# Moving TensorE's operands by 32 bytes, and letting small tiles share memory

## The chip, the cores and the metric

The kernel runs on one NeuronCore of a Trainium2 chip. It is one launch, and the time is the device time of that launch in microseconds (us). Everything is fp32 at the interface.

Five engines work side by side: TensorE (PE in the profile, with its weight loads as PEld), VectorE (DVE), ScalarE (ACT), GpSimd (POOL) and SyncE (SP, which here only issues DMAs). SBUF, the on-chip memory, has 128 partitions. A tile occupies the same bytes of every partition, so "the position of a tile" is one byte number.

## The reference

One layer of a streaming encoder runs over 1024 prompt tokens and 64 sample tokens (T = 1088 columns), with a model width of 1024:

```
xn  = rms_norm(x, g_attn)
rq, rk, rv, rg, sq, sk, sv, ga, gb = split(xn @ w_in)
A   = rms_norm(retention(rope(rq), rope(rk), rv)) * silu(rg) @ w_ret_out     # 4 heads of 256
B   = sliding_window_attention(sq, sk, sv, rel_bias, sinks) @ w_swa_out      # 16 heads of 64
x  += (sigmoid(ga) * A + sigmoid(gb) * B) @ w_mix_out
x  += softmax((rms_norm(x) @ w_cq) @ mk.T) @ mv @ w_co                       # 256 memory tokens
x  += (silu(rms_norm(x) @ w_gate) * (rms_norm(x) @ w_up)) @ w_down           # hidden size 2816
y   = rms_norm(x, g_final)
```

The outputs are `y`, the retention states, the window's keys and values, and the keys and values of the memory tokens (`mk`, `mv`).

## The kernel before, in words

**The matmuls.** Activations lie transposed: 128 features on the partitions, tokens along the columns. A number of fp32 precision is split into two parts, `hi` (rounded by a cast on ScalarE, L123) and `lo = x - hi` (on VectorE, L124). A product is three matmuls: weights' hi by operand's hi, hi by lo, lo by hi (`mm3`, L147 to L151, and `multiply`, L197 to L209). In each, one 128 x 128 block of weights is the stationary operand, loaded by an LDWEIGHTS of its own, and 256 to 384 columns of the operand move past it.

**Two families of tiles feed them.** The weights' parts come from `new_op` (L144): a tile `wq` of 2 x 512 floats, 4096 bytes, with hi in the first half and lo in the second. There are five such buffers in the projection phase and six in the later ones (`self.weights(5)`, `self.weights(6)`), used in turn. The moving operands stand in two rings of eight slots, 2 x 1088 floats or 8704 bytes each (`Ring`, L98): the names `B11` to `B22` and `T1` to `T4` (printed as `B` and `T`), `ret`, `swa`, `mix`, `xc`, `co`, `stage` and `swin` in the profile are all slots of the rings.

**The phases, in order.** The projections run from 0 to about 820 us as Strassen products of 2 x 2 blocks (`strassen`, L247; seven products instead of eight), each product a run of 272-column matmuls. Between them lie the retention of the four heads (`retention`, L702) and, near the end, the memory's keys and values (`memory_phase`, L482). Then come the window attention with `w_ret_out` as filler, `w_swa_out` and `w_mix_out` (320 and 384 columns), cross attention (`w_cq`: 256 and 320 columns), `w_co`, and from about 1500 us the feed-forward network, again as Strassen products of 272 columns. A scheduler orders the instructions of each engine at build time from the dependences between tiles.

**Where the tiles stand.** Pools of the left side are stacked from byte 0 upward, pools of the right side from byte 229344 downward. Every tile takes a multiple of 32 bytes. Before the change:

- the `wq` buffers start at byte 16320 and every 4096 bytes after that, all at a multiple of 64;
- the 16 ring slots start at byte 90080 and every 8704 bytes after that. 90080 = 1407 * 64 + 32, and 8704 = 136 * 64, so all slots stand at byte 32 of 64. Inside a slot the parts used are 1088, 2176 and 4352 bytes apart or start 1024, 1536, 2048 or 3072 bytes in, all multiples of 64, so that every moving operand in the rings starts at byte 32 of 64;
- the retention's operands (`ks`, `qs`, `kt`, `vb`, `ss`, `st`) and cross attention's (`mkv`, `cqs`, `cpT`) are on the left, all at a multiple of 64;
- the memory's operands `ms` are on the right below the rings, at byte 32 of 64;
- `b12`, the block `B12` of the first product of the projections and of the feed-forward network (printed as `b`), is on the left in the first case (byte 45504, a multiple of 64) and on the right in the second (byte 32 of 64).

So the pairs of residues that a matmul meets (moving operand, weights; byte of 64) are (32, 0) for all ring products, (0, 0) in retention and cross attention and for the first `b12`, (32, 0) where `ms` moves past `wq` (`w_mk`) and (0, 32) where `wq` moves past `ms` (`w_mv`; there the weights' tile is the moving operand). Both parts of an operand always have the same residue. In the last phase (`finish`) weights stand in ring slots too (`wb`), which makes (32, 32).

**Room.** In the retention's phase the left side ends at byte 90048 and the rings begin at 90080; in the memory's phase the left side ends at 73664 and `ms` begins at 73696. 32 bytes are free in each.

**The small tiles.** At the end of each head, `retention` handles the 64 sample tokens: it loads keys `kf` (tag `sf`), values `vf` and queries `qf` (tag `qsm`), and keeps a masked score in `sf` (tag `sfs`). `memory_phase` loads the memory's raw columns into `mraw` (two buffers) and puts results into `mo` (four buffers).

Of the kernel before, what the change touches and what calls it, by code (L numbers as in the profile page):

```python
# [11 lines left out]
F32 = mybir.dt.float32  # L12
F32R = mybir.dt.float32r
# [6 lines left out]
P = 128  # L20
# [3 lines left out]
SMP = 64  # L24
# [6 lines left out]
NMEM = 256  # L31
# [78 lines left out]
class Kernel:  # L110
# [31 lines left out]
        return parts  # L142

    def new_op(self):  # L144
        return self.wp.tile([P, 2, 512], F32R, tag="wq", bufs=self.wbufs, name="wq")

    def mm3(self, ps, wh, wl, xh, xl, start, stop):  # L147
        mm = self.nc.tensor.matmul
# [184 lines left out]
    def run(self):  # L333
        nc, tc, io = self.nc, self.tc, self.io
        with ExitStack() as ctx:
            cp = ctx.enter_context(tc.tile_pool(name="const", bufs=1, reuse_waits="tile"))
            self.np = ctx.enter_context(tc.tile_pool(name="norm", bufs=1, reuse_waits="tile"))
            dp = ctx.enter_context(tc.tile_pool(name="scratch", bufs=1, reuse_waits="tile", space=DRAM))

            self.ident = cp.tile([P, P], F32, name="ident")  # L340
            self.ones = cp.tile([P, P], F32, name="ones")
            self.gains = cp.tile([P, 5, KT], F32, name="gains")
            self.load(self.gains, io["g_all"])
            nc.vector.memset(self.ones, 1.0)
            self.rstd = cp.tile([P, T], F32, name="rstd")
            nc.scalar.mul(self.rstd[:, :1], self.ones[:, :1], 1.0)

            self.root = cp.tile([P, len(CH), 3], F32, name="root")
            self.rtok = cp.tile([P, 9], F32, name="rtok")
            nc.vector.memset(self.rtok, 1.0)  # L350
            self.mtok = cp.tile([P, 2], F32, name="mtok")
            self.tab = cp.tile([P, 2, H, 3], F32, name="tab")
            self.tok = cp.tile([P, 3, H, 9], F32, name="tok")
            self.sinks = cp.tile([P, NPAIR], F32, name="sinks")

            self.d_mk = dp.tile([H, P, 2, NMEM], F32, name="d_mk")
            self.d_mv = dp.tile([H, P, 2, NMEM], F32, name="d_mv")
            self.d_ret = dp.tile([KT, P, T], F32, name="d_ret")
            self.d_swa = dp.tile([KT, P, T], F32, name="d_swa")
            self.d_gate = [dp.tile([KT, P, T], F32, name=f"d_gate{i}") for i in range(3)]  # L360
            self.d_mix = dp.tile([KT, P, T], F32, name="d_mix")
            self.d_h = [dp.tile([KT, P, T], F32, name=f"d_h{i}") for i in range(2)]
            self.d_op = dp.tile([len(OPS), FT // 2, P, HALF], F32, name="d_op")
            self.d_rb = dp.tile([16, 64 * 256], F32, name="d_rb")

            self.d_qkv = dp.tile([3, KT, P, T], F32, name="d_qkv")
            self.d_skv = dp.tile([2, P, T], F32, name="d_skv")
            self.d_sq = dp.tile([NPAIR // 2, P, 17, 2, 64], F32, name="d_sq")

            with ExitStack() as sctx:  # L370
                self.rings = [Ring(sctx.enter_context(tc.tile_pool(name=f"ring{i}", bufs=1, reuse_waits="tile", side="right")))
                              for i in range(2)]
                self.mem = sctx.enter_context(ExitStack())
                with self.weights(5):
                    self.project_phase()
                with self.weights(6):
                    with self.plain_psum():
                        self.mix_phase()
                        self.mem.close()
                        self.cross_phase()  # L380
                    rp = sctx.enter_context(tc.tile_pool(name="rf", bufs=1, reuse_waits="tile", side="right"))
                    self.rstd_f = rp.tile([P, T], F32, name="rstd_f")
                    self.temp = sctx.enter_context(ExitStack())
                    self.new_b12(self.temp, side="right")
                    self.cross_out_phase()
                    self.ffn_phase()
# [95 lines left out]
    def memory_phase(self, mp):  # L482


        nc, tc, io = self.nc, self.tc, self.io
        g_mem = self.gains[:, 4, :]
        mr = self.mem.enter_context(tc.tile_pool(name="mr", bufs=1, reuse_waits="tile", side="right"))
        ms = self.ms = [mr.tile([P, 2, NMEM], F32R, name=f"ms{k}") for k in range(KT)]
        macc = mp.tile([P, NMEM], F32, name="macc")
        out = lambda: mp.tile([P, NMEM], F32, tag="mo", bufs=4, name="mo")  # L490
        room = lambda: mp.tile([P, 1024], F32, tag="mw", bufs=3, name="mw")
        for k in range(KT):
            x = mp.tile([P, NMEM], F32, tag="mraw", bufs=2, name="mraw")
            self.load(x, io["memT"][:, k, :])
            self.gained(ms[k], 0, NMEM, x, g_mem, k)
            if k:
                nc.scalar.activation(x, x, AF.Square)
                nc.vector.tensor_tensor(out=macc, in0=macc, in1=x, op=ALU.add)
            else:
                nc.scalar.activation(macc, x, AF.Square)  # L500
            if k % 2:
                yield
        self.token_rstd(self.mtok, [macc], self.spans(NMEM), D)
        yield
        self.spread(macc, self.mtok)
        for m in range(KT):
            ps = self.dense(self.unit(io["w_mk"][m], KT, room=room), ms, 0, NMEM)
            o = out()
            nc.vector.tensor_tensor(out=o, in0=ps, in1=macc, op=ALU.mult)
            self.store(self.d_mk[m // 2, :, m % 2, :], o)  # L510
            self.store(io["o_mk"][m], o)
            yield
        for h in range(H - 1):
            us = [self.unit(io["w_mv"][h, i], 4, 256, room) for i in range(2)]
            for t in range(2):
                ps = self.dense_psum()
                for k in range(KT):
                    x = ms[k][:, :, t * P:(t + 1) * P]
                    self.mm3(ps[:, :256], x[:, 0], x[:, 1], *us[k // 4][k % 4], k == 0, k == KT - 1)
                o = out()  # L520
                nc.scalar.mul(o, ps[:, :256], self.mtok[:, t:t + 1])
                self.store(self.d_mv[h, :, t, :], o)
                self.store(io["o_mv"][t * P:(t + 1) * P, h * 256:(h + 1) * 256], o)
            yield
# [177 lines left out]
    def retention(self, h):  # L702
        nc, io = self.nc, self.io
        mm = nc.tensor.matmul
        ra = self.ra
# [7 lines left out]
        for b in range(NBLK):  # L713
# [28 lines left out]
            sf = ra.tile([P, BLK + P], F32, tag="sf", bufs=1, name="sf")  # L742
# [31 lines left out]
        self.store(io["o_rsp"][h].rearrange("(t p) e -> p t e", p=P), state)  # L774

        s0, vf = new("state"), new("vf")
        kf, qf = (ra.tile([P, 2, SMP], F32, tag=tag, bufs=1, name=tag) for tag in ("sf", "qsm"))
        self.load(s0, io["cstate"][h].rearrange("(t p) e -> p t e", p=P))
        vf = vf[:, :, :SMP]
        for j, x in ((1, kf), (2, vf), (0, qf)):  # L780
# [6 lines left out]
        pss = self.bank("psss")  # L787
        for dt in range(2):
            mm(pss[:SMP, 0, :SMP], kf[:, dt, :], qf[:, dt, :], start=dt == 0, stop=dt == 1)
        sf = ra.tile([P, SMP], F32, tag="sfs", bufs=1, name="sfs")  # L790
        nc.vector.scalar_tensor_tensor(sf[:SMP], pss[:SMP, 0, :SMP], self.rtok[:SMP, 8:], dm[:SMP, BLK + P:],
                                       ALU.mult, ALU.mult)
        po = self.bank("pos")
# [903 lines left out]
```

## Time and profile before

| | |
|---|---|
| median of 3 runs | 2240.6 us (2237.51 to 2248.04) |
| the profiled execution's own time | 2239.58 us |
| its span, first to last instruction | 2237.8 us |
| PE busy | 2171.3 us, 97% of the span |
| DVE, ACT, POOL busy | 72%, 40%, 31% |
| mean granted TensorE clock | 0.986 |

An instruction's row shows its line, engine and operation, then the tiles it writes and reads. For a matmul the PSUM bank stands left of the arrow; right of it the moving operand is named first and the stationary one second. A matmul's duration (about 0.29 us) is longer than the distance to the next one (about 0.12 us), since they are pipelined. The rate at which TensorE works is read from the distance between starts, which the timeline shows with a resolution of 10 ns.

### The profile page before, as it was taken

How to read it: one execution, taken by the hardware profiler on the slowest of the kernel's cores; microseconds unless marked ns; L12 is line 12 of the kernel's file. 1: busy time of each engine (PE TensorE's matmuls, PEld its weight loads, DVE VectorE, ACT ScalarE, POOL GpSimd, SP SyncE). 2: the span in 40 equal slices, each digit the busy share in tenths (PEclk: the TensorE clock that was granted, in tenths of full speed). 3: DMA queues.
4: the chain of work that ended last, by engine and by line, in shares of the span. 5: the costliest groups of instructions: out<-in, count | busy, mean ns of one | idle time of the engine just before them, and what ended most of it. 6: DMA issues, size and time to landing. Idle time of an engine off the chain costs nothing.

```text
span 2237.8 us, 41757 instructions
## 1 busy us (share of the span) xinstructions
PE 2171.3 (97%) x16434; PEld 2106.8 (94%) x16434; DVE 1600.4 (72%) x2655; ACT 884.7 (40%) x1897; POOL 690.5 (31%) x466
## 2 busy tenths in 40 slices
PE   9999999999999989999999999999999999999996
PEld 9899999999999977779999998999999999999986
DVE  8986878676687668876455555668777777778588
ACT  7333333435444355553133333333222222334243
POOL 1441533342253112220000000014555555434462
PEclk9999999999999999999999999999999999999998
DMA  5433345443445475326443112422332332475233
GB/s 205 156 111 110 117 123 137 133 127 113 167 152 178 151 229 169 114 75 208 130 154 107 55 48 65 134 85 88 122 130 101 102 122 89 142 273 182 84 102 109
DMA packets 182599, 290.86 MB, mean 130 GB/s; under 512 B 40290, under 2 KB 110850, under 8 KB 182402
## 3 DMA queue, kind: packets, MB, share of 16 engines
q1 hardware_dynamic: 177794, 279.26, 39.3%
q10 hardware_dynamic: 4608, 8.91, 1.1%
q8 instruction: 130, 2.13, 0.4%
q14 instruction: 67, 0.55, 0.1%
HBM read 196.95 MB, written 91.16 MB: 129 GB/s over the span
## 4 chain that ended last, share of the span: by engine, by line
PE 75%; DVE 7%; DMA 4%; issue 1%; ACT 1%; POOL 1%; SPq 0%; DVEq 0%; ACTq 0%; POOLq 0%
PE pq L208 14%; PE pq L206 14%; PE pq L205 14%; PE pd L149 7%; PE pd L151 7%; PE pd L150 7%; PE pout L1000 1%; DMA hl<-d_op 1%; PE pp L984 1%; DVE wq L124 1%; PE pss L942 1%; DMA ld<-d_swa 1%; DVE B L124 1%; DMA raw<-w_ret_out 1%; PE pk L699 0%
## 5 line engine op out<-in xcount | busy, mean ns | idle before, releaser
L124 DVE TENSOR_TENSOR wq<-raw,wq 128x512 fp32r<-128x512 f32 (+1 forms) x505 | 450.1, 895 | 124.8 <-ACT wq L123 122.6
L123 ACT CAST wq<-raw 128x512 fp32r<-128x512 f32 (+1 forms) x505 | 307.6, 614 | 569.9 <-PE pq L208 262.7
L205 PE MATMUL pq<-T,wq 128*128 128x272 f32 x1832 | 493.9, 289 | 6.2 <-DVE u L252 3.6
L206 PE MATMUL pq<-T,wq 128*128 128x272 f32 x1832 | 493.9, 289 | 0.0
L206 PE MATMUL pq<-B,wq 128*128 128x272 f32 x1592 | 429.3, 289 | 8.4 <-DVE B L124 8.4
L205 PE MATMUL pq<-B,wq 128*128 128x272 f32 x1592 | 426.7, 288 | 0.0
L208 PE MATMUL pq<-T,wq 128*128 128x272 f32 x1832 | 384.4, 290 | 3.4 <-DVE wq L124 3.4
L183 POOL TENSOR_TENSOR raw<-raw 128x512 f32<-128x512 f32 (+1 forms) x59 | 79.4, 1345 | 894.8 <-DVE rs_r L291 483.8
L205 PEld LDWEIGHTS pq<-T,wq 128*128 128x128 f32 x1832 | 346.7, 189 | 7.1 <-DVE u L252 3.7
L206 PEld LDWEIGHTS pq<-T,wq 128*128 128x128 f32 x1832 | 346.8, 189 | 0.3 <-issue 0.3
L208 PE MATMUL pq<-B,wq 128*128 128x272 f32 x1592 | 334.0, 290 | 0.0
L206 PEld LDWEIGHTS pq<-B,wq 128*128 128x128 f32 x1592 | 300.7, 189 | 10.3 <-DVE B L124 10.0
L205 PEld LDWEIGHTS pq<-B,wq 128*128 128x128 f32 x1592 | 300.1, 189 | 0.7 <-issue 0.4
L208 PEld LDWEIGHTS pq<-T,wq 128*128 128x128 f32 x1832 | 292.0, 191 | 4.6 <-DVE wq L124 3.8
L208 PEld LDWEIGHTS pq<-B,wq 128*128 128x128 f32 x1592 | 253.5, 190 | 0.5 <-issue 0.3
L252 DVE TENSOR_TENSOR u<-pq,u 128x544 f32<-128x544 f32 x177 | 127.5, 720 | 111.7 <-PE pq L208 111.1
L186 POOL TENSOR_TENSOR raw<-raw 128x512 f32<-128x512 f32 (+1 forms) x59 | 85.3, 1446 | 125.2 <-DVE wq L124 122.6
L970 POOL TENSOR_TENSOR t<-t,den 128x768 f32<-128x768 f32 (+2 forms) x34 | 47.8, 1406 | 167.7 <-DVE den L968 49.9
L571 DVE TENSOR_TENSOR stage<-pq,u 128x544 f32<-128x544 f32 x112 | 80.3, 717 | 26.6 <-PE pq L208 25.8
L184 POOL TENSOR_TENSOR raw<-raw 128x512 f32<-128x512 f32 (+1 forms) x59 | 89.2, 1512 | 3.7
L1455 POOL TENSOR_TENSOR y<-u,y 128x544 f32<-128x544 f32 x38 | 62.6, 1658 | 72.4 <-DVE y L1453 54.4
L189 POOL TENSOR_TENSOR raw<-raw 128x512 f32<-128x512 f32 (+1 forms) x59 | 83.2, 1411 | 4.4
(373 smaller groups left out, 4674.2 us busy)
## 6 DMA issues: line engine op xcount, KB each, us to landing
hl<-d_op SPq DMA_DIRECT2D x85, 272.0 KB, 4.4
d_qkv<-stage SPq DMA_DIRECT2D x44, 272.0 KB, 2.3
d_op<-stage SPq DMA_DIRECT2D x44, 272.0 KB, 2.1
d_op<-ht SPq DMA_DIRECT2D x44, 272.0 KB, 3.3
raw<-w_gate SPq DMA_DIRECT2D x22, 512.0 KB, 3.5
raw<-w_up SPq DMA_DIRECT2D x22, 512.0 KB, 3.6
d_gate<-stage ACTq DMA_DIRECT2D x32, 272.0 KB, 2.8
raw<-w_down SPq DMA_DIRECT2D x16, 512.0 KB, 4.4
```

The source lines that it names most:

```text
L123: self.last_cast = self.nc.scalar.copy(hi, src).ins
L124: return self.nc.vector.tensor_tensor(out=lo, in0=src, in1=hi.bitcast(F32), op=ALU.subtract).ins
L149: mm(ps, wh, xh, start=start, stop=False)
L150: mm(ps, wh, xl, start=False, stop=False)
L151: self.last_mm = mm(ps, wl, xh, start=False, stop=stop).ins
L184: tt(out=a21, in0=a21, in1=a22, op=add)
L186: tt(out=a11, in0=a22, in1=a11, op=sub)
L189: tt(out=a12, in0=a12, in1=a11, op=sub)
L205: mm(ps[:, c, :HC], w[:, 0, ks], x[:, 0, cs], start=start, stop=False)
L206: mm(ps[:, c, :HC], w[:, 0, ks], x[:, 1, cs], start=False, stop=False)
L208: self.last_mm = mm(ps[:, c, :HC], w[:, 1, ks], x[:, 0, c * HC:(c + 1) * HC], start=False, stop=stop).ins
L252: add = lambda out, a, b: nc.vector.tensor_tensor(out=out, in0=a, in1=b, op=ALU.add)
```

## The change

Three things are done:

1. A tile `edge` of 8 floats (32 bytes) is allocated on the right before the rings and never used. All that lies below it on the right moves down by 32 bytes. The ring slots, `ms` and the second `b12` then start at a multiple of 64.
2. A `wq` buffer becomes 1032 floats (4128 bytes), and the parts start 32 bytes into it. With the first buffer at 16320 the parts start at 16352 (byte 32 of 64), the next at 20480 (byte 0), and so on by turns. The pairs of the ring products become (0, 32) in buffers 0, 2 and 4 and (0, 0) in buffers 1, 3 and 5. What lies above the buffers on the left moves up by 160 bytes with five of them (a residue of 32 instead of 0: retention's operands become (32, 32)) and by 192 bytes with six (residues as before).
3. To make room, `mraw` takes its buffers from `mo`'s four, and `kf`, `qf` and the masked score become parts of one tile `small` under the tag `sf`. That frees 2048 bytes in the memory's phase and 768 in the retention's.

No instruction is added or removed.

```diff
     def new_op(self):
-        return self.wp.tile([P, 2, 512], F32R, tag="wq", bufs=self.wbufs, name="wq")
+        q = self.wp.tile([P, 1032], F32R, tag="wq", bufs=self.wbufs, name="wq")
+        return q[:, 8:8 + 1024].rearrange("p (a b) -> p a b", a=2)
...
             with ExitStack() as sctx:
+                edge = sctx.enter_context(tc.tile_pool(name="edge", bufs=1, reuse_waits="tile", side="right"))
+                edge.tile([P, 8], F32, name="edge")
                 self.rings = [Ring(sctx.enter_context(tc.tile_pool(name=f"ring{i}", bufs=1, reuse_waits="tile", side="right")))
...
         for k in range(KT):
-            x = mp.tile([P, NMEM], F32, tag="mraw", bufs=2, name="mraw")
+            x = mp.tile([P, NMEM], F32, tag="mo", bufs=4, name="mraw")
             self.load(x, io["memT"][:, k, :])
...
         s0, vf = new("state"), new("vf")
-        kf, qf = (ra.tile([P, 2, SMP], F32, tag=tag, bufs=1, name=tag) for tag in ("sf", "qsm"))
+        small = ra.tile([P, 5, SMP], F32, tag="sf", bufs=1, name="small")
+        kf, qf, sf = small[:, :2], small[:, 2:4], small[:, 4]
...
-        sf = ra.tile([P, SMP], F32, tag="sfs", bufs=1, name="sfs")
         nc.vector.scalar_tensor_tensor(sf[:SMP], pss[:SMP, 0, :SMP], self.rtok[:SMP, 8:], dm[:SMP, BLK + P:],
```

## The prediction

> **What bounds the kernel now.** The page comes first: its span, the busy times, the granted clock and the chain that ended last.
>
> ```profile
> span 2237.8 us, 41757 instructions
> PE 2171.3 (97%) x16434; PEld 2106.8 (94%) x16434; DVE 1600.4 (72%) x2655; ACT 884.7 (40%) x1897; POOL 690.5 (31%) x466
> PEclk9999999999999999999999999999999999999998
> PE 75%; DVE 7%; DMA 4%; issue 1%; ACT 1%; POOL 1%; SPq 0%; DVEq 0%; ACTq 0%; POOLq 0%
> ```
>
> TensorE is busy for 97% of the span at a granted clock of 0.9 or more in all slices but the last, and three quarters of the chain are its own instructions. The groups by line, with different shapes kept apart, show which.
>
> ```profile
> L205 PE MATMUL pq<-T,wq 128*128 128x272 f32 x1832 | 493.9, 289 | 6.2 <-DVE u L252 3.6 <-DVE B L124 1.2 <-ACT wq L123 0.8
> L206 PE MATMUL pq<-B,wq 128*128 128x272 f32 x1592 | 429.3, 289 | 8.4 <-DVE B L124 8.4
> L149 PE MATMUL pd<-xc,wq 128*128 128x256 f32 x192 | 54.3, 283 | 0.0
> L149 PE MATMUL pd<-ret,wq 128*128 128x384 f32 x128 | 46.4, 362 | 5.1 <-ACT wq L123 5.1
> L149 PE MATMUL pd<-co,wq 128*128 128x320 f32 x64 | 19.9, 312 | 0.0
> L149 PE MATMUL pd<-ms,wq 128*128 128x256 f32 x64 | 17.9, 280 | 0.0
> L205 PE MATMUL pq<-b,wq 128*128 128x272 f32 x32 | 9.6, 316 | 0.5 <-ACT rstd_f L331 0.5
> ```
>
> Each Strassen matmul occurs once in L205, L206 and L208, so there are 3 x (1832 + 1592 + 32) = 10368 ring products of 272 columns. `xc` adds 3 x 192 = 576 of 256 columns, the four operands `ret`, `swa`, `mix`, `co` give 4 x 3 x 128 = 1536 of 384, and with `xc` 5 x 3 x 64 = 960 of 320. Waits ahead of them are 0 to 8 us a group: the time is the matmuls' own pace. One nanosecond on each of the 10368 is 10.4 us.
>
> What the change can do is therefore read from the pace, that is from starts in the timeline, at stretches with different pairs of residues (moving operand, weights).
>
> ```profile
> 1640.28 0.29 PE L205 MATMUL pq<-T,wq 128*128 128x272 f32 x1
> 1655.21 0.29 PE L205 MATMUL pq<-T,wq 128*128 128x272 f32 x1
> ...
> 35.20 0.29 PE L205 MATMUL pq<-b,wq 128*128 128x272 f32 x1
> 37.46 0.29 PE L206 MATMUL pq<-B,wq 128*128 128x272 f32 x1
> 67.42 0.29 PE L206 MATMUL pq<-B,wq 128*128 128x272 f32 x1
> ...
> 692.09 0.28 PE L149 MATMUL pd<-ms,wq 128*128 128x256 f32 x1
> 695.59 0.28 PE L149 MATMUL pd<-ms,wq 128*128 128x256 f32 x1
> 756.37 0.28 PE L149 MATMUL pd<-wq,ms 128*128 128x256 f32 x1
> 761.34 0.28 PE L149 MATMUL pd<-wq,ms 128*128 128x256 f32 x1
> ...
> 143.29 0.28 PE L149 MATMUL pkv<-vb,kt 128*128 128x256 f32 x1
> 144.60 0.28 PE L151 MATMUL pkv<-vb,kt 128*128 128x256 f32 x1
> ```
>
> In order: 120 ring matmuls of 272 columns with (32, 0) take 14.93 us, 124.4 ns each. The first `b12`, (0, 0), takes 2.26 us for 18, or 125.6; the ring products behind it, (32, 0) again, take 29.96 us for 240, or 124.8. At 256 columns `ms` past `wq`, (32, 0), takes 3.50 us for 30, or 116.7; `wq` past `ms`, (0, 32), takes 4.97 us for 42, or 118.3; the retention's (0, 0) takes 1.31 us for 11, or 119.1. The pair of today is the quickest at both widths.
>
> **The change part by part.** *Ring products, 272 columns.* Their pair goes from (32, 0) to (0, 0) in half of the buffers and (0, 32) in the other half. Equal residues cost 125.6 - 124.8 = 0.8 ns against the same phase's own pace, 1.2 against the later one; I take 0.8, the neighbour with the same work beside it. No row shows (0, 32) at this width. At 256 columns it costs 1.6 where equal residues cost 2.4, two thirds, so I take 0.5 here; the bounds are the most that 256 columns show, 2.4, on the slow side and the same amount below nothing, since nothing excludes a pair quicker than today's. Sum: 5184 x 0.8 + 5184 x 0.5 = 4.1 + 2.6 = 6.7 us.
>
> *The other ring products.* 256 columns (`xc`): 288 x 2.4 + 288 x 1.6 = 1.2 us. 320 and 384 columns, 2496 of them, have only (32, 0) rows; between the mean of 272 columns (0.65) and that of 256 (2.0) I take 1.3, or 3.3 us, with 1.6 and 5.0 as ends. `w_mk` (`ms` past `wq`, 192) goes to (0, 0) and (0, 32): 96 x 2.4 + 96 x 1.6 = 0.4 us. `w_mv` (192) goes from (0, 32) to (32, 0) and (0, 0) by turns: 96 x (-1.6) + 96 x 0.8, nothing. All of this lies on the path: no other engine fills it.
>
> *Retention and `finish`.* Retention's operands go from (0, 0) to (32, 32) and `wb` from (32, 32) to (0, 0): equal before and after. I put nothing on them; cross attention keeps (0, 0).
>
> *Other engines' operands* move by 32 bytes too.
>
> ```profile
> L252 DVE TENSOR_TENSOR u<-pq,u 128x544 f32<-128x544 f32 x177 | 127.5, 720 | 111.7 <-PE pq L208 111.1
> L571 DVE TENSOR_TENSOR stage<-pq,u 128x544 f32<-128x544 f32 x112 | 80.3, 717 | 26.6 <-PE pq L208 25.8 <-ACT ret_o L819 0.7
> ```
>
> `u` stands at byte 0 of 64 and `stage` at byte 32, and the same addition takes 720 and 717 ns. So VectorE shows no price, and none is set; VectorE is busy 72% beside TensorE's 97%, and 3 ns on 289 instructions would be 0.9 us under that cover. If the cover failed it would be 0.9 us.
>
> *Small tiles.* What is queued and who waits:
>
> ```profile
> L117 SPq DMA_DIRECT2D qsm<-d_qkv x4: 360/374/388, 100.4 to 457.8; - x4
> DMA to landing us min/median/max: 2.0/2.5/4.4
> L117 SPq DMA_DIRECT2D sf<-d_qkv x4: 359/360/360, 196.5 to 547.0; - x4
> L789 PE MATMUL psss<-qsm,sf x16: 222/222/270, 211.7 to 563.9; 128*64 128x64 f32 x16
> L117 SPq DMA_DIRECT2D mraw<-memT x8: 328/328/433, 580.4 to 646.2; - x8
> L498 DVE TENSOR_TENSOR macc<-macc,mraw x7: 411/419/1082, 619.0 to 664.7; 128x256 f32<-128x256 f32 x7
> L509 DVE TENSOR_TENSOR mo<-pd,macc x8: 411/424/425, 694.7 to 756.2; 128x256 f32<-128x256 f32 x8
> ```
>
> The sample's queries were loaded early, into a tile of their own (head 0 at 100.4 us). Under the tag `sf` their load waits, like the keys', until the last score tile is free, and stands beside the keys' load on SP's queue, 196.5 us for head 0. With two issues of 0.4 us and the longest landing, 4.4 us, they are there at 201.7; the scores `psss` read them at 211.7. The 10 us between hide it. If that cover went, four heads would pay up to 4.4 us each, 17.6 us. The masked score and the queries now hold the tag longer, but its next user is the next head's first score, behind that head's projections. `mraw` gets four buffers for two, so its loads on SP may go earlier; the first `mo` comes at 694.7, 30 us behind the last reader of `mraw`. Both cost nothing. The order that the scheduler writes may shift by some instructions; I give that plus or minus 3 us.
>
> Sum: 6.7 + 1.2 + 3.3 + 0.4 = 11.6 us. The profiled execution took 2239.6 us, so 2251.2 on it; it stands 1.0 below the median of 2240.6, which gives 2252 us.
>
> *A rule against the whole sum.* The Trainium skill's page "TensorE: Matmul & The Clock Gate", section "Step-by-step: what each phase is for", says that TensorE has two independent SBUF read ports and that loading the next weights takes nothing from the running matmul's reads. By that rule the pair of residues would not matter and the sum would be 0. This trace's 116.7, 118.3 and 119.1 ns at one width speak against it, though they come from different phases.
>
> The same page's section "Back-to-back issue gap" gives N / 2.4 + 2.5 ns for an isolated matmul, which is 115.8 ns at 272 columns as an estimate; the rows show 124.4, and no row here reaches that figure.
>
> **The rivals.** *Only equality counts* (the residue of the moving operand alone is free): half the buffers pay 0.8, the other half nothing, so 4.1 + 0.7 + 1.6 + 0.2 = 6.6 us, 2247 us. For it: at 272 columns only an equal pair is seen to be slower. Against it: (0, 32) is slower than (32, 0) at 256.
>
> *Nothing of it counts.* The paces differ by phase, not by address: right behind `b12`, ring products still run at 124.8, not 124.4. Then 2240 us, within the 3 us of the order. Against it: three steady paces at 256 columns.
>
> *The full price at every width.* 256 columns show 2.4 and 1.6, mean 2.0. On 10368 + 2496 matmuls that is 25.7 us, with 1.6 for `xc` and `w_mk` 27 us: 2268 us. Against it: `b12` at 272 shows only 0.8 to 1.2.
>
> *Faster.* The pair (0, 32) could be quicker at 272 columns than any seen: the operand of 1088 bytes = 17 x 64 begins on a multiple of 64. It decides from the point where the gain of one half of the 12864 wide matmuls outweighs the 0.8 of the other half, that is below 123.6 ns; at 3 ns under today's pace, 121.4, it gives 6432 x (0.8 - 3) = -14 us, 2226 us. For it: paces of one width differ by up to 2.4 ns, so such a step is of the size seen. Against it: (0, 32) at 256 columns is 1.6 ns slower, not quicker.
>
> **How the numbers follow.** 0.5%, about what a measurement of this kernel can tell from no change, is 11.2 us: the bounds are 2229.4 and 2251.8. My forecast gets 0.45 and lies on the upper bound, with 0.27 above and 0.18 below it, since its own range, 2246 to 2260, reaches further up. The full price gets 0.15 (slower), equality alone 0.12 and nothing 0.12 (both within), faster 0.16. So slower 0.42, within 0.42, faster 0.16. The range from 2231 to 2268 holds all but the faster case and a small rest above.
>
> **What would show it.** In the profile after: no new waits ahead of TensorE's groups, and in the feed-forward stretch two paces by turns from product to product, about 125.2 and 124.9 ns instead of 124.4 everywhere. `w_mk` would run at 118.3 or 119.1 by turns of four k's, `w_mv` at 116.7 or 119.1. Retention should stay at 119.1. The prediction fails if a pair that no row shows, (0, 32) at 272 columns or (32, 32) at 256, has a pace of its own outside 122 to 127 ns, if the position within a larger unit than 64 bytes matters (four residues of 128 now occur), or if the queries' load comes late.

## The result and the profile after

The median is 2250.1 us (2245.9 to 2255.2) beside 2242.0 us (2237.5 to 2248.0) for the kernel before in the same series, 14 runs each: ratio 1.0032, 95% interval 1.0023 to 1.0041. So it is slower by 8 us, and that lies within 0.5%. The profiled execution took 2247.5 us with a span of 2245.7, which is 7.9 longer than the span before. The granted clock is the same (0.987 and 0.986).

The page of the kernel after, in the same lines as before (span, busy time of each engine, granted clock in 40 slices, shares of the chain that ended last):

```profile
span 2245.7 us, 41766 instructions
PE 2179.8 (97%) x16434; PEld 2115.3 (94%) x16434; DVE 1596.3 (71%) x2655; ACT 884.2 (39%) x1897; POOL 707.6 (32%) x466
PEclk9999999999999989999999999999999999999998
PE 80%; DVE 10%; DMA 4%; issue 2%; ACT 2%; POOL 2%; SPq 0%; DVEq 0%; ACTq 0%; POOLq 0%
```

PE's busy time grew by 8.5 us, about as much as the span. The nine instructions more (41757 before) all stand on semaphores; the work of each engine has the same count as before. The groups by line of the kernel after (count | busy us, mean ns of one | idle before):

```profile
L206 PE MATMUL pq<-T,wq 128*128 128x272 f32 x1832 | 499.2, 290 | 5.8 <-DVE u L253 3.5 <-DVE B L124 1.1 <-ACT wq L123 0.6
L207 PE MATMUL pq<-B,wq 128*128 128x272 f32 x1592 | 432.4, 290 | 5.3 <-DVE B L124 5.3
L150 PE MATMUL pd<-xc,wq 128*128 128x256 f32 x192 | 54.4, 284 | 0.0
L150 PE MATMUL pd<-co,wq 128*128 128x320 f32 x64 | 19.9, 311 | 0.0
```

The 272-column groups grew: 493.9 to 499.2 us and 429.3 to 432.4. The groups of `xc` (54.3 to 54.4) and of 320 columns (19.9 to 19.9) did not. Idle time ahead of these groups is no more than before. TensorE's waits, by the line that waited and what it waited for (us in all, times, longest), and the rows of the new tile `small`:

```profile
PE pd L150 <- ACT wq L123: 7.1, 2, 5.3
PE pq L207 <- DVE B L124: 5.3, 6, 1.8
...
PE pss L150 <- ACT qs L123: 3.9, 1, 3.9
```

```profile
L793 PE MATMUL psss<-small x16: 221/222/271, 213.2 to 566.2; 128*64 128x64 f32 x16
L117 SPq DMA_DIRECT2D small<-d_qkv x8: 359/408/1497, 198.0 to 549.7; - x8
```

No wait above 1.1 us in all is new. One grew: the retention's scores waited 3.9 us for the split of their queries, where they waited 1.2 before. The sample's loads are issued from 198.0 us for head 0 (queries and keys now share the tile), the scores start at 213.2 us, and no wait on them stands among TensorE's waits.

The pace itself is read from the timeline. These rows are the first matmuls of nine products in a row in the feed-forward stretch, 24 matmuls of 272 columns each (start us, us, engine, line):

```profile
1700.72 0.28 PE L206 MATMUL pq<-T,wq 128*128 128x272 f32 x1
1703.71 0.29 PE L206 MATMUL pq<-T,wq 128*128 128x272 f32 x1
1706.73 0.29 PE L206 MATMUL pq<-T,wq 128*128 128x272 f32 x1
1709.75 0.28 PE L206 MATMUL pq<-B,wq 128*128 128x272 f32 x1
1712.76 0.29 PE L206 MATMUL pq<-T,wq 128*128 128x272 f32 x1
1715.78 0.29 PE L206 MATMUL pq<-B,wq 128*128 128x272 f32 x1
1718.82 0.29 PE L206 MATMUL pq<-B,wq 128*128 128x272 f32 x1
1721.80 0.29 PE L206 MATMUL pq<-T,wq 128*128 128x272 f32 x1
1724.82 0.28 PE L206 MATMUL pq<-T,wq 128*128 128x272 f32 x1
```

Their differences over 24 are 124.6, 125.8, 125.8, 125.4, 125.8, 126.7, 124.2 and 125.8 ns: not two paces by turns, but several. Before, all products of this stretch ran at 124.4. The program's addresses say which buffer each product read. The two at 124.6 and 124.2 read the buffer at byte 128 of 256, the one at 126.7 the buffer at byte 224 of 256. Those at byte 128 have the same residue of 64 as those at bytes 0 and 64 of 256 (125.4 and 125.8). So 64 bytes is not the unit in which the pace repeats.

A sum over all distances between starts of the trace (those short enough to be the pace of their width; a longer one counts with the usual pace, and its excess as a stall behind the matmul that it starts from) shows where the time lies:

| us | before | after | difference |
|---|---|---|---|
| 272 columns, ring past `wq` | 1292.4 | 1301.0 | +8.6 |
| 384 columns | 266.8 | 268.2 | +1.4 |
| 320 columns | 140.8 | 140.8 | 0 |
| 256 columns with `wq` (`xc`, `w_mk`, `w_mv`) | 112.9 | 113.4 | +0.5 |
| 256 columns without `wq` (retention, cross attention) | 125.9 | 125.8 | -0.1 |
| 272 columns past other weights | 18.1 | 18.0 | -0.1 |
| stalls behind 272 columns past `wq` | 47.5 | 43.7 | -3.8 |
| stalls behind all the others | 26.7 | 30.3 | +3.6 |
| plain fp32 matmuls and what lies between them | 191.1 | 188.8 | -2.3 |

The differences sum to +7.8, between the first matmul's start and the last one's.

### The profile page after: what moved, and what is told of

It reads as the page before. It is cut to its first block, busy times and chain, and to the rows that moved or that the text cites. A ratio compares the mean times of both kernels' runs of the same rounds, so it can differ in the third digit from the quotient of the medians.

```text
span 2245.7 us, 41766 instructions
## 1 busy us (share of the span) xinstructions
PE 2179.8 (97%) x16434; PEld 2115.3 (94%) x16434; DVE 1596.3 (71%) x2655; ACT 884.2 (39%) x1897; POOL 707.6 (32%) x466
## 4 chain that ended last, share of the span: by engine, by line
PE 80%; DVE 10%; DMA 4%; issue 2%; ACT 2%; POOL 2%; SPq 0%; DVEq 0%; ACTq 0%; POOLq 0%
PE pq L209 15%; PE pq L207 15%; PE pq L206 15%; PE pd L150 8%; PE pd L152 8%; PE pd L151 8%; DVE wq L124 2%; PE pout L1003 1%; PE pp L987 1%; DMA hl<-d_op 1%; POOL raw L184 1%; PE pss L945 1%; DMA qs<-d_qkv 1%; DMA swin<-d_gate 1%; DVE stage L574 1%
## 5 line engine op out<-in xcount | busy, mean ns | idle before, releaser
L206 PE MATMUL pq<-T,wq 128*128 128x272 f32 x1832 | 499.2, 290 | 5.8 <-DVE u L253 3.5
L207 PE MATMUL pq<-B,wq 128*128 128x272 f32 x1592 | 432.4, 290 | 5.3 <-DVE B L124 5.3
L184 POOL TENSOR_TENSOR raw<-raw 128x512 f32<-128x512 f32 (+1 forms) x59 | 99.4, 1685 | 896.5 <-DVE rs_r L292 484.9
L187 POOL TENSOR_TENSOR raw<-raw 128x512 f32<-128x512 f32 (+1 forms) x59 | 82.9, 1404 | 109.3 <-DVE wq L124 106.6
L185 POOL TENSOR_TENSOR raw<-raw 128x512 f32<-128x512 f32 (+1 forms) x59 | 87.6, 1485 | 3.7
L190 POOL TENSOR_TENSOR raw<-raw 128x512 f32<-128x512 f32 (+1 forms) x59 | 83.2, 1411 | 4.4
```

Source lines behind the costliest of these rows:

```text
L184: tt(out=a11, in0=a11, in1=a21, op=sub)
L185: tt(out=a21, in0=a21, in1=a22, op=add)
L206: mm(ps[:, c, :HC], w[:, 0, ks], x[:, 0, cs], start=start, stop=False)
L207: mm(ps[:, c, :HC], w[:, 0, ks], x[:, 1, cs], start=False, stop=False)
```

## The experiments

Two theories stood at the start. The first is the prediction's: the pair of residues modulo 64 sets the pace. The second is its caveat: the position within a larger unit does. Below, d is the address of the moving operand minus that of the weights, modulo 256 bytes, at the start of a product. Before, the ring stands at byte 224 of 256 and every `wq` buffer at 192, so d = 32. The operands of a product's other matmuls start 64, 128 and 192 bytes of 256 past the first one's. So d names a layout, and every product meets four distances: d, d + 64, d + 128 and d + 192. The layouts with d = 32, 96, 160 and 224 meet the same four and differ in how often and in what order. "Early" is the projections, "late" the feed-forward network.

**One part alone.** `rings_only` keeps the edge of 32 bytes and nothing else; the order of instructions is that of before on every engine.

```diff
+                edge = sctx.enter_context(tc.tile_pool(name="edge", bufs=1, reuse_waits="tile", side="right"))
+                edge.tile([P, 8], F32, name="edge")
```

> The 32 bytes before the rings alone; weights and small tiles as before; every engine's instructions stand in the order of the kernel before. All ring products meet (0, 0). If the pair decides and any pair but (32, 0) is slower: 272 columns at 125.1 to 125.6 ns instead of 124.5, so 10368 x 0.6 to 1.1 = 6 to 11 us, and 384 columns 1 ns slower, 1.5 us: a ratio of 1.003 to 1.006. If only weights at byte 32 cost something (the moving operand's byte is free): 124.5 ns and 1.000. If the small tiles or the order of the instructions made the 8 us: 1.000.

`weights_only` leaves the rings where they were and keeps the rest.

```diff
-        return self.wp.tile([P, 2, 512], F32R, tag="wq", bufs=self.wbufs, name="wq")
+        q = self.wp.tile([P, 1032], F32R, tag="wq", bufs=self.wbufs, name="wq")
+        return q[:, 8:8 + 1024].rearrange("p (a b) -> p a b", a=2)
...
-            x = mp.tile([P, NMEM], F32, tag="mraw", bufs=2, name="mraw")
+            x = mp.tile([P, NMEM], F32, tag="mo", bufs=4, name="mraw")
...
+        small = ra.tile([P, 5, SMP], F32, tag="sf", bufs=1, name="small")
...
```

> The wider weight buffers and the shared small tiles, no move of the rings: the pairs are (32, 32) and (32, 0) by turns. If the pair decides: products with weights at byte 0 stay at 124.5 ns, those at byte 32 run at about 125.6, so about 5460 x 1.1 = 6 us, a ratio of 1.002 to 1.004. If the moving operand's byte alone decides: 124.5 ns in both and 1.000. If the turning itself costs: both kinds of product are slower.

`small_only` has the shared small tiles alone.

```diff
-            x = mp.tile([P, NMEM], F32, tag="mraw", bufs=2, name="mraw")
+            x = mp.tile([P, NMEM], F32, tag="mo", bufs=4, name="mraw")
...
-        kf, qf = (ra.tile([P, 2, SMP], F32, tag=tag, bufs=1, name=tag) for tag in ("sf", "qsm"))
+        small = ra.tile([P, 5, SMP], F32, tag="sf", bufs=1, name="small")
+        kf, qf, sf = small[:, :2], small[:, 2:4], small[:, 4]
```

> The shared small tiles alone, all operands of the ring products where they were. If they cost nothing, as I put it: a ratio of 1.000, within 0.001 (3 us for the order of instructions is 0.0013). If the queries' later load is what costs: up to 17.6 us, 1.008, with waits ahead of the sample's scores.

`all32` is the changed kernel with buffers of 1040 floats instead of 1032, so that all of them start at byte 32 of 64.

```diff
-        q = self.wp.tile([P, 1032], F32R, tag="wq", bufs=self.wbufs, name="wq")
+        q = self.wp.tile([P, 1040], F32R, tag="wq", bufs=self.wbufs, name="wq")
```

> Buffers of 1040 instead of 1032 floats: as the change, but every weight part at byte 32, so that all ring products meet (0, 32). If the pair decides and (0, 32) is the slower half, as the changed kernel's trace has it (125.6 ns): 10368 x 1.1 = 11 us and 2 us from the other widths, a ratio of 1.005 to 1.006. If equal residues were the slow half and the turns hid a quick (0, 32): below 1.002.

| | ratio to before | 95% interval |
|---|---|---|
| `rings_only` | 1.0040 | 1.0027 to 1.0052 |
| `weights_only` | 1.0053 | 1.0040 to 1.0067 |
| `small_only` | 1.0005 | 0.9997 to 1.0014 |
| `all32` | 1.0042 | 1.0028 to 1.0055 |

The small tiles cost nothing that the whole time shows, though they change the order of instructions. The retention's wait of 3.9 us comes with them: it is 3.4 to 3.9 us in every run that shares the tiles (3.6 in `small_only`) and 1.3 in `rings_only`. Each of the two shifts alone costs about as much as the whole change: the parts don't add up, as a price on the relation between two operands would have it. The timelines of the first two, starts of products in the feed-forward stretch, `rings_only` (the first matmul of a product and the one 192 later) and then `weights_only` (four products in a row):

```profile
1700.86 0.29 PE L205 MATMUL pq<-B,wq 128*128 128x272 f32 x1
1724.96 0.29 PE L205 MATMUL pq<-T,wq 128*128 128x272 f32 x1
```

```profile
1704.72 0.28 PE L206 MATMUL pq<-T,wq 128*128 128x272 f32 x1
1707.76 0.29 PE L206 MATMUL pq<-T,wq 128*128 128x272 f32 x1
1710.77 0.29 PE L206 MATMUL pq<-T,wq 128*128 128x272 f32 x1
1713.79 0.29 PE L206 MATMUL pq<-B,wq 128*128 128x272 f32 x1
```

`rings_only`, pair (0, 0) throughout, runs at 24.10 / 192 = 125.5 ns. That is the prediction's pace for equal residues, 125.6. But the three products of `weights_only` read buffers at bytes 128, 32 and 64 of 256 beside a ring at 224. The first and the third have the pair (32, 0) of the kernel before, and they take 126.7 and 125.8 ns instead of 124.4; the second, an equal pair, takes 125.4. Over all late products of `weights_only` the three buffers with (32, 0) average 125.5 (byte 0 of 256), 125.7 (byte 64) and 126.0 (byte 128). So the pair alone does not set the pace. This run leaves one other reading, which its expectation names: that turning from buffer to buffer costs something by itself. The next runs take the turns away.

**One d for all buffers.** To see each d by itself, the buffers were left 4096 bytes apart, all equal modulo 256, and moved together by a pad that nothing uses. The small tiles are shared as in the change, the rings unmoved. `shift_224` moves all buffers by 224 bytes, d = 64; the others move them by two values, one for the projections (five buffers) and one for what comes later (six).

```diff
     def new_op(self):
+        if self.pad:
+            self.wp.tile([P, self.pad // 4], F32, tag="pad", bufs=1, name="pad")
+            self.pad = 0
         return self.wp.tile([P, 2, 512], F32R, tag="wq", bufs=self.wbufs, name="wq")
...
+        self.pad = {5: 224, 6: 224}[bufs]
```

> Weight buffers 4096 bytes apart as before, but all moved up by 224 bytes; rings as before; small tiles shared. Every ring product meets (32, 32). If the byte of 64 decides: 125.5 ns at 272 columns everywhere, as the half of weights_only with weights at byte 32, so about +10 us, 1.004. If the distance between operand and weights counts in a larger unit than 64 bytes (224 - 160 = 64 of 256, the distance of the one class of the changed kernel that ran at 124.4): 124.4 ns or below and 1.000 or below.

`shift_96_64`:

```diff
-        self.pad = {5: 224, 6: 224}[bufs]
+        self.pad = {5: 96, 6: 64}[bufs]
```

> All weight buffers moved up by 96 bytes in the projections and by 64 bytes from the window attention on, 4096 bytes apart. Projections meet (32, 32), the rest (32, 0) as before. If the byte of 64 decides: 125.5 ns early, and 124.5 ns in the feed-forward network, the pace of before. If a larger unit counts: the feed-forward network, now at a distance of 224 of 256 instead of 32, runs near the 125.5 ns that weights_only showed at this distance. If only the mixing of places between buffers costs, and one place for all is free of it: 124.5 in both.

`shift_160_128`:

```diff
-        self.pad = {5: 224, 6: 224}[bufs]
+        self.pad = {5: 160, 6: 128}[bufs]
```

> All weight buffers moved up by 160 bytes in the projections and by 128 from the window attention on. Projections meet (32, 32), the rest (32, 0). If the byte of 64 decides: 125.5 early and 124.5 late. If a larger unit counts: late at a distance of 160 of 256, where weights_only showed 125.7.

`shift_32_192`:

```diff
-        self.pad = {5: 224, 6: 224}[bufs]
+        self.pad = {5: 32, 6: 192}[bufs]
```

> All weight buffers moved up by 32 bytes in the projections and by 192 from the window attention on. Early the distance is 0, as in rings_only, with both operands 32 bytes higher: 125.6 if the distance alone decides. Late the pair is (32, 0) at a distance of 96 of 256: 124.5 if the byte of 64 decides, about 126 if the larger unit does, as weights_only showed there.

Starts in the feed-forward stretch, the first matmul of a product and the one 192 later, of `shift_224`, `shift_96_64`, `shift_160_128` and `shift_32_192`; the last fence adds one product of the projections of `shift_32_192` (24 matmuls):

```profile
1702.68 0.28 PE L208 MATMUL pq<-B,wq 128*128 128x272 f32 x1
1726.47 0.28 PE L208 MATMUL pq<-T,wq 128*128 128x272 f32 x1
```

```profile
1703.01 0.29 PE L208 MATMUL pq<-T,wq 128*128 128x272 f32 x1
1727.33 0.29 PE L208 MATMUL pq<-T,wq 128*128 128x272 f32 x1
```

```profile
1700.12 0.29 PE L208 MATMUL pq<-T,wq 128*128 128x272 f32 x1
1724.22 0.29 PE L208 MATMUL pq<-T,wq 128*128 128x272 f32 x1
```

```profile
1701.32 0.29 PE L208 MATMUL pq<-B,wq 128*128 128x272 f32 x1
1725.32 0.29 PE L208 MATMUL pq<-T,wq 128*128 128x272 f32 x1
...
117.39 0.29 PE L208 MATMUL pq<-B,wq 128*128 128x272 f32 x1
120.40 0.29 PE L208 MATMUL pq<-T,wq 128*128 128x272 f32 x1
```

Over 192 they are 123.9, 126.7, 125.5 and 125.0 ns. Of these four only `shift_224` has in this stretch an equal pair of 64, (32, 32), and it is the quickest; the other three all have the pair (32, 0) of before and are all slower than 124.4. Here the theory of 64 bytes falls, and without turns between buffers. Averages over all undisturbed products of the layouts (24 matmuls with no distance above 0.2 us), with the ratio of the whole kernel:

| d, bytes of 256 | from | ns per matmul | ratio to before |
|---|---|---|---|
| 64 | `shift_224`, late | 123.9 | 0.9971 (0.9958 to 0.9983) |
| 32 | before | 124.5 | 1 |
| 96 | `shift_32_192`, late | 125.1 | 1.0047 (1.0028 to 1.0065), early part at d = 0 |
| 192 | `shift_96_64`, early | 125.4 | see 224 |
| 128 | `shift_160_128`, early | 125.4 | see 160 |
| 160 | `shift_160_128`, late | 125.6 | 1.0031 (1.0020 to 1.0043) |
| 0 | `rings_only` | 125.6 | 1.0040 |
| 224 | `shift_96_64`, late | 126.4 | 1.0044 (1.0029 to 1.0059) |

That the distance counts and not the two places has one direct test here: the projections of `shift_32_192` have d = 0 with both operands at byte 224 of 256, `rings_only` has it with both at byte 192. The rows give 3.01 / 24 = 125.4 and 125.5; the averages over all products are 125.6 in both.

The d does not fix the pace in every layout. The late part of `shift_96_64` (d = 224) runs at 126.7 ns up to a break, and at 125.6 from there on, with weights and operands at the same places of 256. The break is 3 us long: matmuls of neighbouring products alternate, and one waits. These rows are that wait and two starts behind it, 192 matmuls apart:

```profile
1982.28 0.40 PE L209 MATMUL pq<-B,wq 128*128 128x272 f32 x1 [0.20 <-DVE B L124]
...
1989.16 0.29 PE L208 MATMUL pq<-B,wq 128*128 128x272 f32 x1
...
2013.27 0.29 PE L208 MATMUL pq<-B,wq 128*128 128x272 f32 x1
```

Over 192 that is 125.6 ns. The 126.4 of the table is the mean of both paces. The late part of `shift_32_192` goes from 125.0 to 125.6 at three waits of 0.4 to 1.3 us between 2065 and 2070 us; one of 0.45 us at 1980 left its pace as it was. The early parts at d = 128 and 192 vary too (124.4 to 126.0 and 125.0 to 125.8). Only d = 0, 32, 64 and 160 keep one pace nearly throughout.

**TensorE alone.** `pace` takes everything else away: one operand past another, 48 matmuls per stretch, each with a weight load of its own, at distances 16 bytes apart. It was run once.

```diff
+        def stretch(n, xr, d):
...
+            ps = pp.tile([P, 512], F32, tag="p", name=f"n{n}x{xr}d{d}s")
...
+                for i in range(COUNT):
+                    xa = 64 * (i % 3) + xr // 4
+                    wa = 128 * (i % 4) + (xr - d) % 256 // 4
+                    last = mm(ps[:, :n], w[:, wa:wa + P], x[:, xa:xa + n], start=i == 0, stop=i == COUNT - 1).ins
```

> Leaves out the whole layer: TensorE alone runs stretches of 48 matmuls of one width, each with a fresh block of weights, and nothing else touches memory meanwhile. The distance d between moving operand and weights (bytes of 256) is the same within a stretch and runs from 0 to 240 in steps of 16, at 256, 272, 320 and 384 columns; at 272 columns it is repeated with both operands 32 and 96 bytes higher. If the pace hangs on the distance in a unit of 256 bytes: at 256 columns it ranges from about 113 ns (seen in shift_96_64 and shift_224 at d = 192) to 120 ns (d = 0), and the repeats at 272 columns agree with the first within 1 ns. If the places themselves count, or other engines' accesses make the spread: the repeats differ, or all stretches of one width run alike.

The timeline of `pace` (start us, us of the whole stretch; the name of the bank carries width, shift of both operands and distance):

```profile
46.64 5.92 PE L73 MATMUL n256x0d96s<-x,w 128*128 128x256 f32 x48
52.39 5.91 PE L73 MATMUL n256x0d112s<-x,w 128*128 128x256 f32 x48
...
80.98 5.62 PE L73 MATMUL n256x0d192s<-x,w 128*128 128x256 f32 x48
86.44 5.82 PE L73 MATMUL n256x0d208s<-x,w 128*128 128x256 f32 x48
...
127.61 6.24 PE L73 MATMUL n272x0d64s<-x,w 128*128 128x272 f32 x48
133.69 6.24 PE L73 MATMUL n272x0d80s<-x,w 128*128 128x272 f32 x48
...
175.85 6.09 PE L73 MATMUL n272x0d192s<-x,w 128*128 128x272 f32 x48
181.78 6.13 PE L73 MATMUL n272x0d208s<-x,w 128*128 128x272 f32 x48
...
482.58 6.09 PE L73 MATMUL n272x32d192s<-x,w 128*128 128x272 f32 x48
530.78 6.09 PE L73 MATMUL n272x96d192s<-x,w 128*128 128x272 f32 x48
```

From one stretch's first start to the next's, over 48: 256 columns take 119.8 ns at d = 96 and 113.8 at 192; 272 columns take 126.7 at d = 64 and 123.5 at 192. The last two rows have both operands 32 and 96 bytes further at d = 192, and the same 6.09 us as without. Once a stretch has settled (from its 17th matmul on), the means are 113.3 to 120.1 ns at 256 columns, 123.3 to 126.7 at 272, 144.5 to 146.7 at 320 (146.7 at all but two of sixteen distances) and 173.3 to 176.7 at 384. With both operands moved by 32 and 96 bytes, seven of the eight distances that were tried at 272 columns repeat to 0.4 ns; d = 96 alone gives 125.5 twice and 126.7 once.

With nothing else running, then, the pace depends on the distance between the two operands. The Trainium skill's page "TensorE: Matmul & The Clock Gate", section "Step-by-step: what each phase is for", says that TensorE has two independent SBUF read ports and that a weight load takes nothing from the running matmul. 113.3 beside 120.1 ns at one width in this run does not fit that, as far as the pace is concerned.

The map at 272 columns is not that of the kernel: d = 64 is the slowest here and the quickest there. Two differences are on record: other engines work beside TensorE in the kernel, and a product mixes four distances while a stretch of `pace` keeps one. That the mixture accounts for it was not shown, and a plain mean does not: of six matmuls two meet d, two d + 64, one d + 128 and one d + 192. At d = 64, with the settled means of `pace` (126.7, 126.7, 123.3 and 125.4 ns at d = 64, 128, 192 and 0), that gives 125.9 as an estimate, where `shift_224` ran at 123.9.

**A layout from the map.** `placed` is `shift_224` with gaps that bring the 256-column pairs without `wq` to d = 192, the quickest of the map; `shift_224_again` ran beside it on the same chip.

```diff
+    def gap(self, pool, size):
+        self.gaps = getattr(self, "gaps", 0) + 1
+        pool.tile([P, size // 4], F32, tag=f"gap{self.gaps}", bufs=1, name="gap")
...
+                if t == 0 and k in (1, 2):
+                    self.gap(self.ra, (0, 192, 64)[k])
...
-            ks, qs, vf = pair("ks"), pair("qs"), new("vf")
+            if h == 0 and b == 0:
+                self.gap(ra, 128)
+            ks = pair("ks")
+            if h == 0 and b == 0:
+                self.gap(ra, 192)
+            qs, vf = pair("qs"), new("vf")
...
+                    if h == 0 and c0 == 0:
+                        self.gap(cp, 64)
```

> As shift_224, and gaps of 64 to 192 bytes so that retention's and cross attention's operand pairs, 1056 matmuls of 256 columns, stand at a distance of 192 of 256 instead of 0. The order of instructions is that of shift_224. If the distance sets the pace, as the stretches of pace say (113.3 ns at 192, 120.0 at 0): retention and cross attention near 113 to 115 ns instead of 118.4 to 119.7, 1056 x 5 = 5 us off shift_224, a ratio to the kernel before of 0.994 to 0.996. If retention is held by its chain of splits and transposes and not by TensorE's pace: the paces fall and the time stays at shift_224's 0.997. If the stretches' map does not carry over to mixed work: paces as before.

> shift_224 once more, on the chip of the run beside it, for the comparison of the two: 0.997, between 0.9958 and 0.9983.

`placed` came to 0.9964 (0.9949 to 0.9978), `shift_224_again` to 0.9967 (0.9957 to 0.9977): both faster than before, and not separable from each other. In the trace the retention's and cross attention's matmuls of 256 columns did get quicker, from averages of 118.4 to 119.4 ns by group to 116.0 to 117.5, 2.6 us in all, somewhat under half of what 113.3 would give. (192 of them, cross attention's last product, stood at 128 before and not at 0 as expected.) The median moved by 0.8 us, less than these runs can tell.

The page of `shift_224`, faster than both kernels by its interval:

```profile
span 2235.1 us, 41765 instructions
PE 2162.5 (97%) x16434; PEld 2098.0 (94%) x16434; DVE 1599.0 (72%) x2655; ACT 884.6 (40%) x1897; POOL 690.7 (31%) x466
```

PE's busy time is 8.8 us below before and 17.3 below after, with the same 16434 matmuls. By the same sum as above its 272-column pace takes 1286.6 us, 5.8 less than before.

## Why the prediction was right or wrong

It forecast 2252 us, 11.4 above the kernel before, on the very bound of 0.5%, with equal chances for slower than that and for within it. The result is 2250.1, 8 above the kernel before and within; it lies in the range, and slower is the way that was forecast. Much of the closeness is luck, since the mechanism was only half right and errors cancel in part: 1.9 us too little at 272 columns, 3.0 too much at the other widths, and 2.5 given back that the sum did not have.

- *What bounds the kernel.* Right. The time is TensorE's own pace, and the change is a change of that pace: +8.6 us on 272 columns where the whole is +7.8, with no new wait above 1.1 us.
- *The unit.* Wrong, and this is the step that failed: the pace is not set by the pair of residues of 64. `weights_only` and the three shifts with the pair (32, 0) show paces from 125.1 to 126.4 for the pair that was the quickest at 124.5; `shift_224` shows an equal pair as the quickest of all. Where all buffers share one place of 256, the pace goes with d modulo 256, apart from the layouts that have two paces. The prediction's rows could not tell the two apart, since each pair stood in them at one d only: (32, 0) at 32, (0, 0) at 0, (0, 32) at 224. It named a larger unit as what would break it, and gave it no chance in the rivals.
- *272 columns, 6.7 us.* It measured 8.6. For (0, 0) 0.8 ns was near by luck: products on those buffers average 125.2 late, weighted by count, but as the mean of unlike places (bytes 0, 64 and 128 of 256: 125.4, 125.6, 124.4). For (0, 32), 0.5 was too little: bytes 32, 96 and 224 give 125.7, 125.6 and 125.8, or 1.2 above 124.5. The order was the other way round, and one value for (0, 0) hides a spread of 1.3 ns.
- *A mixed layout is not a mean of uniform ones.* In `all32` the buffers with d = 32, the d of before, run at 125.5 late and not at 124.5, while those with d = 224 run at 125.5 and not at 126.4. So something besides a product's own d matters. What ran just before is the likely one, since the pace of `shift_96_64` changed at a break with every place unchanged; that it is the neighbour's place was not shown. In the changed kernel the average of the uniform paces over its six distances, (126.4 + 125.4 + 125.6 + 125.4 + 125.1 + 123.9) / 6 = 125.3, is nevertheless near the 125.4 measured.
- *320 and 384 columns, 3.3 us.* It measured 1.4, all of it at 384. At 320 columns `pace` shows 146.7 at nearly every distance; the interpolation between 256 and 272 had no basis.
- *`xc`, `w_mk`, `w_mv`, 1.6 us.* It measured 0.5.
- *Retention, cross attention: nothing.* Right (-0.1 us): both operands moved together, so their distance stayed.
- *Small tiles and the queries' load: nothing.* Right in the whole: 1.0005, no wait on the load. The wait of the retention's scores that grew by 2.2 to 2.7 us lies within the 3 us that were given to the order.
- *Given back.* Not in the sum: 3.8 us less stalls behind 272 columns, against 3.6 more elsewhere, and 2.3 us at the plain fp32 matmuls. Of +10.3 us of pace, 7.8 are left. `rings_only`, where the order of instructions is unchanged, also gives back 2.4 us at the fp32 matmuls; why wasn't tried.
- *The rivals.* "Nothing counts" falls with every run but `small_only`. "Only equality counts" falls with `weights_only` and `shift_224`. The full price at every width falls on 320 columns. The faster rival was right in that a quicker layout exists, but it is d = 64 and not the pair (0, 32), and it is 0.5 ns quicker, not 3.
- *The rule against the whole sum* would have given 0. The result, and `pace` above all, speak against it.

Open stays what below the distance makes the pace: which reads meet which, why some distances have two steady paces and a break can change one for the other, and how the four distances within a product combine. Distances finer than 32 bytes in the kernel, and a layout in which all quarters of a product have one distance, weren't tried.

## What to carry to other kernels

Where TensorE's own pace bounds a kernel and each matmul loads its weights, read the distance between starts in the timeline by layout, and vary the relative position of the two operands by a pad before arguing about alignment: here it moved the pace by 2% between best and worst, at no instruction. A rule taken from one or two layouts (here a residue of 64) should be tried on a third that it says is equal, which is one run. Layouts in which all buffers of a ring have the same place modulo 256 are also easier to read, but half of those tried here had more than one pace: read it on both sides of a break before calling it the layout's.

## What the runs showed of the hardware

- The pace of a matmul with a fresh weight load depends on the distance modulo 256 bytes between moving operand and weights, with TensorE alone at work: 113.3 to 120.1 ns at 256 columns, 123.3 to 126.7 at 272, 173.3 to 176.7 at 384, and at 320 only for two of sixteen distances (144.5 and 145.5 beside 146.7).
- The kernel before stood at the second best of the eight values of d tried, without its code saying so.
- Some distances have two steady paces (272 columns, d = 96, TensorE alone: 125.5 and 126.7 in stretches of the same distance). In the kernel the layout with d = 224 went from 126.7 to 125.6 at a break of 3 us and stayed there. With buffers at different places, products leave the pace that their d has in a uniform layout (d = 32: 125.5 in `all32`, 124.5 before).
